# Moving the low-part subtraction of the expert weights from GpSimd to VectorE, and projecting the queries with split weights

## The chip, the core and the metric

The kernel runs on one core of one Trainium2 chip. Five engines work side by side, each through its own queue in order: TensorE (PE; its weight loads are listed apart, as PEld), VectorE (DVE), ScalarE (ACT), GpSimd (POOL) and SyncE (SP), which here only issues DMAs. The metric is the time of one execution in microseconds; lower is better.

## The reference, cut to what matters

Two transformer blocks are computed for 512 tokens of width 1024 in float32. The change is in the last part of the second one, `peer_ffn`, a layer with 16384 experts of one hidden unit each:

```python
q = _rms((xt @ w_q).reshape(T, P_HEADS, P_KEY_DIM)).astype(x.dtype)
s1 = jnp.einsum('thd,hnd->thn', q[..., :half], sub_keys[:, 0])
s2 = jnp.einsum('thd,hnd->thn', q[..., half:], sub_keys[:, 1])
v1, i1 = lax.top_k(s1, P_TOPK)
v2, i2 = lax.top_k(s2, P_TOPK)
cand = (v1[..., :, None] + v2[..., None, :]).reshape(T, P_HEADS, P_TOPK * P_TOPK)
vals, ci = lax.top_k(cand, P_TOPK)
...
a = jnp.einsum('cd,ckd->ck', xc, expert_u[ec])
w = (gc * jax.nn.gelu(a.astype(jnp.float32))).astype(x.dtype)
return jnp.einsum('ck,ckd->cd', w, expert_v[ec])
```

Each token has 8 heads x 16 chosen experts; the rows of expert_u and expert_v that they name are used.

## The kernel before, in words

Float32 weights are multiplied in two parts. `chunk` loads a 128x1024 tile of weights (`wraw`, three buffers), ACT copies it into a reduced format (`whi`, two buffers), and `wlo`, also with two buffers, takes what is left, wraw - whi: one subtraction, on DVE or on POOL by `lo_engine`. `mm3` then makes three matmuls of one product: whi with the high part of the activations, whi with their low part, wlo with the high part (lines L84 to L86). `up_tile` does this for one tile of expert_u ("pu", the first product, 128 experts): 24 matmuls of 384 columns, then Gelu on ACT.

`peer` has three stages that matter here.

- The queries (about 1012 to 1217 us): 16 half heads n. Query n is projected (`w3[n]`), copied by ACT, multiplied with its keys, and DVE searches the 16 best of each row (`top16`); after every second one, POOL and DVE form pairs and decode them (`pairs`, `decode`). From n = 4 on, tiles of the first product stand between the queries, two and one in turn, their low parts by POOL. Only query 0 is projected from split weights. For the others POOL adds the two parts of the activations into `whole` at the start, and the loaded weights are multiplied with it as they are (L1397).
- The gates (about 1217 to 1431): 30 further tiles of the first product, with one-hot matmuls between them that spread the gates of tokens 0 to 383 over all experts.
- The last stage (1431 to the end): step e of 128 multiplies tile e of expert_v ("pv", the second product, 18 matmuls of 512 columns into y) with the gated hidden values. In the first 80 steps a tile of the first product follows each. Beside this runs the work for the last 128 tokens, `gathered`: 256 rows-by-index DMAs (128 from expert_u, "pun", and 128 from expert_v) that POOL issues (L1493) into four buffers (`r4`), each of them then reduced or added by one DVE operation (L1498 for the first 128, L1508 for the rest).

The order of the instructions on every engine is set by a scheduler that simulates the engines. `fetch` puts each gather behind `self.pool_last`, the last subtraction that POOL was given, so that between 80 subtractions on POOL stand the gathers of each step.

Of the kernel before, what the change touches and what calls it, by code (L numbers as in the profile page):

```python
# [12 lines left out]
F32 = mybir.dt.float32  # L13
# [5 lines left out]
ALU = mybir.AluOpType  # L19
# [25 lines left out]
class Builder:  # L45
# [1200 lines left out]
    def peer(self, hd, xn, xd):  # L1246


        nc, tc, bp = self.nc, self.tc, self.bp
        NT = 384  # L1250
        AHEAD = 27
        AWAY = 21
        NREST = 4
        with ExitStack() as s5:
# [3 lines left out]
            T = lambda tag, bufs=1, dt=F32, shape=(128, 512): wk.tile(list(shape), dt, tag=tag, name=tag, bufs=bufs)  # L1258
# [4 lines left out]
            w3 = self.i["w3"]  # L1263
# [12 lines left out]
            def top16(out, ind, s, n):  # L1276
                rest = T("rest", NREST, shape=(128, 128))[:, :n]
                nc.vector.max(out[:, 0:8], s)
                nc.vector.match_replace(rest, out[:, 0:8], s, LOWEST)
                nc.vector.max(out[:, 8:16], rest)  # L1280
                nc.vector.max_index(ind[:, 0:8], out[:, 0:8], s)
                nc.vector.max_index(ind[:, 8:16], out[:, 8:16], rest)
# [16 lines left out]
            def pairs(hd8):  # L1299
                cand = T("oh2", 4, shape=(128, 4, 128))[:, :, :NC]  # L1300
                i = 0
                while i < 16:
                    m, n = sum(r == ROWS[i] for r in ROWS), ROWS[i]
                    sh = [128, 4, m, n]
                    v1 = val[:, :, hd8, 0, i:i + m]
                    v2 = val[:, :, hd8, 1, 0:n]
                    o = cand[:, :, START[i]:START[i] + m * n]
                    if m == 1:
                        v1 = v1.to_broadcast([128, 4, n])
                    elif n == 1:  # L1310
                        v2 = v2.to_broadcast([128, 4, m])
                    else:
                        o = o.rearrange("p b (m n) -> p b m n", n=n)
                        v1, v2 = v1[:, :, :, None].to_broadcast(sh), v2[:, :, None, :].to_broadcast(sh)
                    nc.gpsimd.tensor_tensor(o, v1, v2, op=ALU.add)
                    i += m
                for b in range(4):
                    top16(best[:, b, hd8], ci[:, b, hd8], cand[:, b], NC)
# [44 lines left out]
            def up_tile(e, lo_engine="pool"):  # L1363
                c = self.chunk(self.i["pu"][e], lo_engine=lo_engine)
                p = P()
                for k in range(8):
                    s = slice(k * 128, (k + 1) * 128)
                    self.mm3(p[:, :NT], (c[0][:, s], c[1][:, s]), (xn[0][k][:, :NT], xn[1][k][:, :NT]), k == 0, k == 7)
                away = e >= 128 - AWAY
                g = T("gs", 2, shape=(128, NT)) if away else T("gt", AHEAD, shape=(128, NT))  # L1370
                nc.scalar.activation(g, p[:, :NT], AF.Gelu_apprx_tanh)
                if away:
                    nc.sync.dma_start(ud[e - 128 + AWAY], g)
                else:
                    up[e] = g

            first_tiles = iter([*range(128 - AWAY, 128), *range(AHEAD)])


            whole = T("big", 2, shape=(128, 8, 512))  # L1380
            for k in range(8):
                nc.gpsimd.tensor_tensor(whole[:, k], xn[0][k], xn[1][k], op=ALU.add)

            for n in range(16):
                hd8, half = n // 2, n % 2
                with self.in_order(self.after if n < 2 else []):
                    if n % 4 == 0:
                        keys = T("r4", 4, shape=(128, 2, 512))[:, 0]
                        nc.sync.dma_start(keys, self.i["keys"][n // 4])
                    acc = P()  # L1390
                    if n == 0:
                        self.project(acc, self.chunk(w3[n], lo_engine="pool"), xn)
                    else:
                        w = self.wp.tile([128, 1024], F32, tag="wraw", name="wraw", bufs=3)
                        nc.sync.dma_start(w, w3[n])
                        for k in range(8):
                            nc.tensor.matmul(acc, w[:, k * 128:(k + 1) * 128], whole[:, k], start=k == 0, stop=k == 7)  # L1397
                q = T("r4", 4, shape=(128, 2, 512))[:, 0]
                nc.scalar.copy(q, acc)
                before, sq = sq, TP()  # L1400
                nc.scalar.activation(sq, acc, AF.Square)
                sp = P(f"y{(0, 1, 3, 4, 5)[n % 5]}")
                ks = slice(n % 4 * 128, n % 4 * 128 + 128)
                for b in range(4):
                    bs = slice(b * 128, b * 128 + 128)
                    nc.tensor.matmul(sp[:, bs], q[:, bs], keys[:, ks], start=True, stop=True)
                for b in range(4):
                    top16(val[:, b, hd8, half], idx[:, b, hd8, half], sp[:, b * 128:(b + 1) * 128], 128)
                if half == 1:
                    nc.gpsimd.tensor_tensor(sq, sq, before, op=ALU.add)  # L1410
                    for b in range(4):
                        nc.tensor.matmul(sv[:, b, hd8], sq[:, b * 128:(b + 1) * 128], self.ones[:, 0:2], start=True, stop=True)
                    pairs(hd8)
                    decode(hd8)
                for _ in range((0, 0, 0, 0, 2, 1)[min(n, 4 + n % 2)]):
                    up_tile(next(first_tiles))
# [116 lines left out]
            for e in range(128):  # L1533
                if e % 4 == 0:
                    w = T("big", 2, shape=(128, NT // 32, 4, 32))
                    n = NT // 32 - (e == 0)
                    load = nc.sync.dma_start(w[:, :n], wd[:n, :, e:e + 4, :].rearrange("g p e t -> p g e t"))
                    if e == 0:
                        with tc.issue_after(load.ins):
                            nc.sync.dma_start(wd[n], last[0])  # L1540
                c = self.chunk(self.i["pv"][e])
                hm = TP()[:, :NT]
                hv, uv = (t.rearrange("p (a t) -> p a t", t=32) for t in (hm, up[e]))
                nc.vector.tensor_tensor(hv[:, :n], uv[:, :n], w[:, :n, e % 4], op=ALU.mult)  # L1544
                if e < 4:
                    nc.vector.tensor_tensor(hv[:, n], uv[:, n], last[0][:, e], op=ALU.mult)
                del up[e]
                xh, xl = TP(F32R)[:, :NT], TP(F32R)[:, :NT]
                self.split_into(hm, xh, xl)
                for b in range(3):  # L1550
                    bs = slice(b * 128, b * 128 + 128)
                    for d in range(2):
                        cs = slice(d * 512, d * 512 + 512)
                        self.mm3(y[b][d], (xh[:, bs], xl[:, bs]), (c[0][:, cs], c[1][:, cs]), e == 0, e == 127)
                if e + AHEAD < both:
                    up_tile(e + AHEAD)
                if e + 2 >= both and e + 2 < 128:
                    up[e + 2] = T("gl", 3, shape=(128, NT))
                    nc.sync.dma_start(up[e + 2], ud[e + 2 - both])
                steps = both - AHEAD  # L1560
                work.advance((e + 1) / steps * 0.86 if e < steps else 0.86 + (e + 1 - steps) / 36 * 0.15)
# [106 lines left out]
```

## Time and profile before

| | us |
|---|---|
| three runs | 2383.24, 2383.82, 2390.1 (median 2383.82) |
| profiled execution | 2386.1 |
| its span, first to last instruction | 2384.1 |
| PE busy | 2261.5 (95%) |
| PE weight loads busy | 1906.0 (80%) |
| DVE busy | 1682.8 (71%) |
| POOL busy | 1001.5 (42%) |
| ACT busy | 1003.6 (42%) |
| mean rate of the DMAs | 182 GB/s; in the last stage near 290 |

PE's busy time is nearly the whole span, but it is made of stages with different limits, so the shares by themselves don't say what bounds one of them.

### The profile page before, as it was taken

How to read it: one execution, taken by the hardware profiler on the slowest of the kernel's cores; microseconds unless marked ns; L12 is line 12 of the kernel's file. 1: busy time of each engine (PE TensorE's matmuls, PEld its weight loads, DVE VectorE, ACT ScalarE, POOL GpSimd, SP SyncE). 2: the span in 40 equal slices, each digit the busy share in tenths (PEclk: the TensorE clock that was granted, in tenths of full speed). 3: DMA queues.
4: the chain of work that ended last, by engine and by line, in shares of the span. 5: the costliest groups of instructions: out<-in, count | busy, mean ns of one | idle time of the engine just before them, and what ended most of it. 6: DMA issues, size and time to landing. Idle time of an engine off the chain costs nothing.

```text
span 2384.1 us, 31933 instructions
## 1 busy us (share of the span) xinstructions
PE 2261.5 (95%) x11207; PEld 1906.0 (80%) x11207; DVE 1682.8 (71%) x3504; ACT 1003.6 (42%) x1766; POOL 1001.5 (42%) x829
## 2 busy tenths in 40 slices
PE   6999999999998889899999998999999999999999
PEld 4888888888886668767789998888888878877787
DVE  7766666533457887676789966777767877778875
ACT  4544444422344688622238762333333333323332
POOL 4221121000034657455520006767777767776410
PEclk9999999999999999899999999999999999999999
DMA  3222222333342122333345558988888988889984
GB/s 116 80 82 87 80 80 88 125 94 94 96 126 75 54 71 98 120 97 118 116 135 199 208 196 292 313 297 284 286 290 296 305 281 281 296 281 325 348 306 154
DMA packets 166833, 433.26 MB, mean 182 GB/s; under 512 B 14608, under 2 KB 69392, under 8 KB 165136
## 3 DMA queue, kind: packets, MB, share of 16 engines
q1 hardware_dynamic: 129808, 296.98, 38.5%
q0 software_dynamic: 36864, 134.23, 16.0%
q8 instruction: 88, 1.44, 0.3%
q14 instruction: 73, 0.60, 0.1%
HBM read 391.91 MB, written 38.21 MB: 180 GB/s over the span
## 4 chain that ended last, share of the span: by engine, by line
PE 70%; DVE 10%; DMA 9%; issue 5%; POOL 4%; ACT 2%; DVEq 0%; SPq 0%; POOLq 0%; ACTq 0%
PE mm L86 11%; PE mm L84 10%; PE mm L85 10%; DMA r<-pun_in,row 6%; PE y L85 4%; PE y L86 4%; PE y L1466 4%; PE mm L1397 3%; PE y L84 3%; POOL wlo L71 3%; PE g L86 2%; PE g L85 2%; PE g L84 2%; PE s L367 2%; DMA r<-pv_in,row 2%
## 5 line engine op out<-in xcount | busy, mean ns | idle before, releaser
L65 ACT CAST whi<-wraw 128x1024 fp32r<-128x1024 f32 (+2 forms) x398 | 414.1, 1041 | 742.3 <-PE y L86 281.3
L71 POOL TENSOR_TENSOR wlo<-wraw,whi 128x1024 fp32r<-128x1024 f32 (+3 forms) x124 | 311.6, 2514 | 649.7 <-ACT whi L65 648.5
L86 PE MATMUL mm<-uh,wlo 128*128 128x384 f32 (+1 forms) x1512 | 543.7, 360 | 6.8 <-POOL wlo L71 5.0
L84 PE MATMUL mm<-uh,whi 128*128 128x384 f32 (+1 forms) x1512 | 545.5, 361 | 4.4 <-ACT whi L65 4.1
L85 PE MATMUL mm<-ul,whi 128*128 128x384 f32 (+1 forms) x1512 | 539.9, 357 | 3.6 <-DVE ul L71 3.6
L71 DVE TENSOR_TENSOR wlo<-wraw,whi 128x1024 fp32r<-128x1024 f32 (+1 forms) x274 | 341.6, 1247 | 180.3 <-ACT whi L65 180.1
L85 PE MATMUL y<-wlo,p 128*128 128x512 f32 x768 | 306.9, 400 | 48.2 <-DVE wlo L71 48.0
L86 PEld LDWEIGHTS mm<-uh,wlo 128*128 128x128 f32 x1512 | 285.6, 189 | 36.4 <-POOL wlo L71 17.0
L84 PEld LDWEIGHTS mm<-uh,whi 128*128 128x128 f32 x1512 | 286.1, 189 | 29.8 <-ACT whi L65 4.5
L85 PEld LDWEIGHTS mm<-ul,whi 128*128 128x128 f32 x1512 | 286.0, 189 | 28.3 <-DVE ul L71 3.8
L1498 DVE CUSTOM_DVE_ANT_0 r<-r,val 128x1024 f32<-128x1024 f32 x128 | 226.2, 1783 | 110.0 <-DMA r<-pun_in,row 109.1
L86 PE MATMUL y<-whi,p 128*128 128x512 f32 x768 | 301.3, 393 | 0.0
L1508 DVE SCALAR_TENSOR_TENSOR idx<-r,act,idx 128x1024 f32<-128x1024 f32 x127 | 211.0, 1661 | 76.4 <-DMA r<-pv_in,row 74.9
L1493 POOL DMA_INDIRECT r<-pv_in,row x128 | 189.7, 1482 | 81.4 <-DVE idx L1508 44.7
L85 PEld LDWEIGHTS y<-wlo,p 128*128 128x128 f32 x768 | 144.8, 189 | 97.8 <-DVE wlo L71 67.4
L1493 POOL DMA_INDIRECT r<-pun_in,row x128 | 187.5, 1465 | 42.2 <-issue 20.6
L84 PE MATMUL y<-whi,p 128*128 128x512 f32 x768 | 197.6, 392 | 0.0
L65 ACT CAST p<-p 128x384 fp32r<-128x384 f32 x128 | 65.8, 514 | 292.3 <-DVE p L1544 290.7
L86 PEld LDWEIGHTS y<-whi,p 128*128 128x128 f32 x768 | 144.9, 189 | 30.0
L84 PEld LDWEIGHTS y<-whi,p 128*128 128x128 f32 x768 | 143.0, 188 | 25.3 <-ACT whi L65 0.5
L372 ACT ACTIVATE p<-p,st 128x128 f32<-128x128 f32 (+3 forms) x160 | 89.6, 561 | 71.5 <-DVE st L371 70.6
L1463 DVE TENSOR_SCALAR r<-iota,iT,iT 128x128 f32<-128x128 f32 x384 | 104.6, 342 | 19.9 <-PE y L1466 19.9
(605 smaller groups left out, 3763.0 us busy)
## 6 DMA issues: line engine op xcount, KB each, us to landing
wraw<-w_in SPq DMA_DIRECT2D x145, 512.0 KB, 3.5
wraw<-pu_in SPq DMA_DIRECT2D x128, 512.0 KB, 5.5
wraw<-pv_in SPq DMA_DIRECT2D x128, 512.0 KB, 5.0
wd<-big SPq DMA_DIRECT2D x12, 2048.0 KB, 7.3
big<-wd SPq DMA_DIRECT2D x31, 768.0 KB, 6.1
hd<-h SPq DMA_DIRECT2D x24, 256.0 KB, 2.2
h<-hd SPq DMA_DIRECT2D x16, 256.0 KB, 3.7
ud<-gs SPq DMA_DIRECT2D x21, 192.0 KB, 2.0
```

Of the source, the lines that this page charges most:

```text
L65: nc.scalar.copy(hi, src)
L71: i = eng.tensor_tensor(lo, src, hi, op=ALU.subtract)
L84: mm(out, w[0], x[0], start=start, stop=False)
L85: mm(out, w[0], x[1], start=False, stop=False)
L86: mm(out, w[1], x[0], start=False, stop=stop)
L372: nc.scalar.activation(pi, pi, AF.Exp, bias=st[:, 0:1], scale=-1.0, accum_out=st[:, 1:2])
L1397: nc.tensor.matmul(acc, w[:, k * 128:(k + 1) * 128], whole[:, k], start=k == 0, stop=k == 7)
L1463: nc.vector.tensor_scalar(hot[:, 0, t], iota, i1, g, op0=ALU.is_equal, op1=ALU.mult)
L1466: nc.tensor.matmul(wp[:, t * 128:(t + 1) * 128], hot[:, 0, t], hot[:, 1, t], start=True, stop=True)
L1493: nc.gpsimd.indirect_dma_start(t, None, src, bass.IndirectOffsetOnAxis(ap=rows[n][:, s:s + 1], axis=0))
L1498: nc.vector.tensor_tensor_reduce(t, t, xn3, 1.0, 0.0, ALU.mult, ALU.add, act[:, s:s + 1])
L1508: nc.vector.scalar_tensor_tensor(yg[0], t, act[:, s:s + 1], yg[0], op0=ALU.mult, op1=ALU.add)
```

## The change

In the last stage the subtraction for the first product's tiles goes to DVE. All 16 queries are projected from split weights, with the low part on POOL for queries 0 and 1 and on DVE for the others; `whole`, its eight additions and the matmuls with whole weights go.

```diff
-            whole = T("big", 2, shape=(128, 8, 512))
-            for k in range(8):
-                nc.gpsimd.tensor_tensor(whole[:, k], xn[0][k], xn[1][k], op=ALU.add)
...
                     acc = P()
-                    if n == 0:
-                        self.project(acc, self.chunk(w3[n], lo_engine="pool"), xn)
-                    else:
-                        w = self.wp.tile([128, 1024], F32, tag="wraw", name="wraw", bufs=3)
-                        nc.sync.dma_start(w, w3[n])
-                        for k in range(8):
-                            nc.tensor.matmul(acc, w[:, k * 128:(k + 1) * 128], whole[:, k], start=k == 0, stop=k == 7)
+                    self.project(acc, self.chunk(w3[n], lo_engine="pool" if n < 2 else "dve"), xn)
...
                 if e + AHEAD < both:
-                    up_tile(e + AHEAD)
+                    up_tile(e + AHEAD, "dve")
```

The scheduler orders all engines anew. Three places show it; in the changed kernel L1482 is the gather that was L1493, L1487 the operation that was L1498, L1533 the product of hidden values and gates that was L1544, L1526 and L1529 are the loads and the last store of the gates that were L1537 and L1540.

POOL's queue early in the last stage, before:

```order
L1493 DMA r_13877<-pun_in,row_13505 128x1024
L1493 DMA r_13880<-pun_in,row_13505 128x1024
L1493 DMA r_13883<-pun_in,row_13505 128x1024
L71 TENSOR_TENSOR wlo<-wraw,whi 128x1024
L1493 DMA r_13949<-pun_in,row_13505 128x1024
L1493 DMA r_13952<-pun_in,row_13505 128x1024
L1493 DMA r_13955<-pun_in,row_13505 128x1024
L71 TENSOR_TENSOR wlo<-wraw,whi 128x1024
```

The same queue of the changed kernel:

```order
L1482 DMA r_14168<-pun_in,row_13796 128x1024
L1482 DMA r_14171<-pun_in,row_13796 128x1024
L1482 DMA r_14174<-pun_in,row_13796 128x1024
L1482 DMA r_14240<-pun_in,row_13796 128x1024
L1482 DMA r_14243<-pun_in,row_13796 128x1024
```

The subtractions are gone and with them the place that bound a gather to its step; gathers follow each other.

DVE's queue in the middle of the gathers from expert_u, about one step of the last stage, before (one wlo a step, for pv; the rows that write only act read out a sum; p<-gt,big makes the hidden values, p<-p their low part):

```order
L71 TENSOR_TENSOR wlo<-wraw,whi 128x1024
L1498 ISA r_14956,act<-r_14956,val 128x1024
L1498 ISA act 128x1
L1498 ISA r_14959,act<-r_14959,val 128x1024
L1498 ISA act 128x1
L71 TENSOR_TENSOR p<-p 128x384
L1544 TENSOR_TENSOR p<-gt,big 128x384
```

The same of the changed kernel:

```order
L71 TENSOR_TENSOR wlo<-wraw,whi 128x1024
L1487 ISA r_15824,act<-r_15824,val 128x1024
L1487 ISA act 128x1
L71 TENSOR_TENSOR wlo<-wraw,whi 128x1024
L1487 ISA r_15890,act<-r_15890,val 128x1024
L1487 ISA act 128x1
L71 TENSOR_TENSOR p<-p 128x384
L1533 TENSOR_TENSOR p<-gt,big 128x384
L1487 ISA r_15893,act<-r_15893,val 128x1024
```

A second subtraction per step, for pu, stands between the gather operations, most with one of them ahead of it.

SP's queue where the last stage begins, before (wd holds the gates in memory; big is a tile of them for four steps):

```order
L1540 DMA wd<-big 128x4096
L94 DMA wraw<-pv_in 128x1024
L1537 DMA big<-wd 128x12x128 x2
L94 DMA wraw<-pu_in 128x1024
L94 DMA wraw<-pv_in 128x1024
```

The same of the changed kernel:

```order
L1529 DMA wd<-big 128x4096
L94 DMA wraw<-pv_in 128x1024
L94 DMA wraw<-pu_in 128x1024
L1526 DMA big<-wd 128x12x128 x2
L94 DMA wraw<-pv_in 128x1024
```

One load of pu weights has moved ahead of the two loads of gates.

## Rows read from the trace of the kernel before

**Rows 1.** Busy time by stretch: length, PE, PEld, DVE, ACT, POOL, clock, DMA, GB/s.

```profile
1012.00:1217.00 205.00, 202.16 (x858) 142.30 (x857) 149.48 (x793) 46.40 (x69) 105.40 (x111) 0.99 0.35 110
1217.00:1431.00 214.00, 214.00 (x1516) 213.81 (x1515) 184.89 (x566) 149.74 (x266) 7.65 (x11) 1.00 0.55 194
1500.00:2150.00 650.00, 603.89 (x2954) 528.61 (x2953) 493.40 (x519) 208.14 (x283) 470.89 (x264) 1.00 0.87 291
2200.00:2300.00 100.00, 97.76 (x423) 78.72 (x422) 83.51 (x100) 35.77 (x48) 39.99 (x26) 1.00 0.96 342
```

**Rows 2.** Instructions of line 84: duration min/median/max in ns, first and last start.

```profile
L84 PE MATMUL mm<-uh,whi x1512: 331/335/795, 39.9 to 2172.9; 128*128 128x384 f32 x128, 128*128 128x512 f32 x61
...
L84 PE MATMUL y<-whi,p x768: 387/392/498, 1431.5 to 2375.3; 128*128 128x512 f32 x192
```

**Rows 3.** The chain that ended last: start, us, what.

```profile
1119.95 6.87 PE mm L1397 x16
...
2304.28 1.37 PE y L84 x6
2308.40 1.37 PE y L84 x6
```

**Rows 4.** Timeline of PE in one tile of the first product, every third matmul.

```profile
1966.76 0.33 PE L86 MATMUL mm<-uh,wlo 128*128 128x384 f32 x1
...
1967.28 0.33 PE L86 MATMUL mm<-uh,wlo 128*128 128x384 f32 x1
```

**Rows 5.** Waits from 1432 to 2190: total us, times, longest.

```profile
POOL wlo L71 <- ACT whi L65: 318.3, 47, 188.1
...
DVE r L1498 <- DMA r<-pun_in,row: 109.1, 64, 6.2
DVE idx L1508 <- DMA r<-pv_in,row: 71.9, 44, 3.5
PEld y L85 <- DVE wlo L71: 62.3, 39, 2.7
...
PEld mm L86 <- POOL wlo L71: 17.0, 34, 1.9
```

**Rows 6.** Groups by line from 1432 to 2190: busy us, mean ns, idle before.

```profile
L71 POOL TENSOR_TENSOR wlo<-wraw,whi 128x1024 fp32r<-128x1024 f32 x80 | 213.4, 2668 | 319.5 <-ACT whi L65 318.3
```

**Rows 7.** Instructions of line 1498: duration min/median/max in ns.

```profile
L1498 DVE CUSTOM_DVE_ANT_0 r<-r,val x128: 1209/1226/3623, 1441.9 to 1870.0; 128x1024 f32<-128x1024 f32 x128
```

**Rows 8.** Groups by line from 2195 to 2300, after the first product's last tile.

```profile
L1508 DVE SCALAR_TENSOR_TENSOR idx<-r,act,idx 128x1024 f32<-128x1024 f32 x31 | 39.6, 1279 | 3.0 <-DMA r<-pv_in,row 3.0
```

**Rows 9.** Costliest groups of the whole span, from the page.

```profile
L1498 DVE CUSTOM_DVE_ANT_0 r<-r,val 128x1024 f32<-128x1024 f32 x128 | 226.2, 1783 | 110.0 <-DMA r<-pun_in,row 109.1
...
L1508 DVE SCALAR_TENSOR_TENSOR idx<-r,act,idx 128x1024 f32<-128x1024 f32 x127 | 211.0, 1661 | 76.4 <-DMA r<-pv_in,row 74.9
```

**Rows 10.** Timeline of POOL and DVE at two places: start, us, instruction.

```profile
1475.53 3.62 DVE L1498 CUSTOM_DVE_ANT_0 r<-r,val 128x1024 f32<-128x1024 f32 x1 [0.71 <-DMA r<-pun_in,row]
1475.64 2.43 POOL L71 TENSOR_TENSOR wlo<-wraw,whi 128x1024 fp32r<-128x1024 f32 x1
...
1966.46 1.21 DVE L71 TENSOR_TENSOR wlo<-wraw,whi 128x1024 fp32r<-128x1024 f32 x1
1966.74 1.74 POOL L1493 DMA_INDIRECT r<-pv_in,row  x1 [0.30 <-DVE p L1544]
1968.79 0.94 POOL L1493 DMA_INDIRECT r<-pv_in,row  x1 [0.31 <-PE mm L86]
```

**Rows 11.** DMA issues, 1431 to 2190, then 2195 to 2290: median us to landing.

```profile
r<-pun_in,row POOLq DMA_INDIRECT x128, 6.6
...
r<-pv_in,row POOLq DMA_INDIRECT x28, 8.5
```

**Rows 12.** Timeline of ACT where the last stage begins.

```profile
1456.32 1.04 ACT L65 CAST whi<-wraw 128x1024 fp32r<-128x1024 f32 x1 [6.22 <-DMA wraw<-pu_in]
```

**Rows 13.** Groups by line while the queries are projected, 1012 to 1217.

```profile
L71 POOL TENSOR_TENSOR wlo<-wraw,whi 128x1024 fp32r<-128x1024 f32 x18 | 42.5, 2364 | 26.3 <-ACT whi L65 26.3
```

## The prediction

> **What bounds the kernel now.** I read stretches first, then the waits inside the stretch that the change touches. In each row of [rows 1] stand the length, the busy us of TensorE (PE), of its weight loads, VectorE (DVE), ScalarE (ACT) and GpSimd (POOL), then granted clock, DMA share and GB/s. Where the queries are projected (1012 to 1217 us) PE is busy 202 of 205 us; in the next stage (1217 to 1431), which the change leaves alone, 214 of 214. So a microsecond that PE saves on the queries ends the stage after it a microsecond sooner, as long as nothing else becomes late.
>
> The last stage begins with the first product into y at 1431.5. Its first 80 steps each hold 24 matmuls of 384 columns (one tile of the first product, "pu") and 18 of 512 columns (one of the second, "pv"); the last pu matmul is at 2172.9 [rows 2]. That is 741.7 us, 9.27 a step. What PE needs for a step: six matmuls of 512 columns take 1.37 us in the chain, 18 take 4.11 (an undisturbed pv step late in the kernel goes from 2304.28 to 2308.40, 4.12) [rows 3]; three of 384 columns take 0.52 [rows 4], 24 take 4.16. Together 8.27, for 80 steps 662 us. So 80 us of these steps are not matmul pace. PE is in fact busy only 604 of 650 us there, and at 291 GB/s and 0.87 of the DMA engines the memory isn't full either [rows 1].
>
> Who keeps PE waiting stands in the waits of this stretch [rows 5]: first DVE's low part of the pv weights, 62.3 us at the weight loads; POOL's low part of the pu weights, 17.0. DVE is late because of the gathers: it stood 109.1 and 71.9 us waiting for gathered rows. These are late because POOL, which issues them in order with its 80 subtractions, stood 318.3 us before a subtraction whose ScalarE copy wasn't there (188 of it one wait ahead of the stage), with gathers behind it in its queue. And each subtraction is long: 2.67 us [rows 6].
>
> The second loss is a collision. The gather operation of the first half of DVE's list (L1498) has a median of 1.226 us [rows 7], that of the second (L1508) takes 1.279 late in the stage, where POOL only issues [rows 8]; their means over the stage are 1.783 and 1.661 [rows 9]. The differences, 0.56 and 0.38 us, times 128 and 127, are 120 us of DVE time. One pair shows where it goes: L1498 takes 3.62 us from 1475.53, and POOL's 2.43 us subtraction begins in it at 1475.64 [rows 10]: 1.21 us of work and 2.41 of standing.
>
> **The change, the last stage.** POOL loses 80 subtractions, 213 us [rows 6], and nothing of POOL's is left between gathers: as the order shows, they follow each other. DVE gains 80 subtractions of 1.21 us [rows 10], 97 us, and gets back up to 120 us of standing, as POOL's remaining work there is issuing, beside which L1508 takes its 1.279 us [rows 8].
>
> DVE's step is then (counted in DVE's order, 230 gather operations stand ahead of the 80th step's end, where 209 stood: 2.88 a step) 2.88 x 1.31 (L1498 with its 0.08 us read-out), two subtractions, 2.42, and two short operations of 0.55: 7.3 us, 88% of PE's 8.27. It fits, but PE's pu weights now stand in the same queue as the gathers.
>
> Whether the gathers come in time: four r buffers go round. Now a round takes 4 x 741.7/209 = 14.2 us. Without POOL's subtractions it is an issue of 1.74 us when DVE is busy (0.94 when idle) [rows 10], a landing of 6.6 us, or 8.5 as it was late in the stage at a DMA share of 0.96 [rows 1, 11], DVE's 1.3, and 0.3 between issues: 9.9 to 11.8. At 2.88 gathers a step that asks for 7.1 to 8.5 us a step. So PE's 8.27 and the ring's 8.5 are nearly the same, and nothing else asks for more: 2.75 MB a step (two weight tiles, a quarter of a 768 KB load, 2.88 gathers of 512 KB) at the 342 GB/s of [rows 1] are 8.0 us.
>
> Bounds for a step: 8.27 below; above, 9.27 plus what it costs if the pu weights come as late as the pv weights do (62.3 us in place of POOL's 17.0): 9.83. I take 8.45, by the row that it is nearest to: 2200 to 2300, where DVE already makes every low part at the same pace of a chunk each 4.1 us, DMA is at 0.96, and PE is busy 97.8% [rows 1]; 8.27/0.978 = 8.46. Of the start of the stage I keep 4 us: PE stood there while ScalarE waited for a pu weight load until 1456.32 (6.2 us) [rows 12]; SP now issues one pu load ahead of two large loads, which may shorten it. 80 x 8.45 + 4 = 680 against 741.7: -62 us (bounds -80 and +45). The remaining 48 pv steps ran from 2173 to just past 2375.3 [rows 2], 4.2 a step against 4.12; they have 25 gathers now instead of 46: -2 us.
>
> **The change, the queries.** A whole-weight product of one query is 16 pieces and 6.87 us in the chain [rows 3]; split, it is 24 matmuls at 1.37/6, 5.48. Fifteen times 1.39 is 20.9 us of PE saved. Added are 15 copies of 1.04 us on ACT (46 of 205 us busy), 14 subtractions of 1.21 on DVE (149 of 205) and one on POOL, less eight additions there: each has room [rows 1]. But the queries now share the two whi and two wlo buffers with the pu tiles between them, where before they took none. A copy can begin only when the tile before the preceding one is multiplied, so copy and subtraction must fit in the preceding tile's 4.16 us: 1.04 + 1.21 on DVE does, 1.04 + 2.36 on POOL [rows 13] just does, if neither stands in its queue; ahead of DVE's now stand top-16 searches, ahead of POOL's the decoding. Fully covered: -20.9. Nothing covered: 15 x 2.25 = 34 on top, +13. I take -13, nearer to the covered end, since both sums fit into 4.16 us and DVE would be at 166 of 187 us.
>
> The sum: -62 - 2 - 13 = -77. The profiled execution took 2386.1 us (span 2384.1 and 2.0 around it), 2.3 over the median of 2383.8; from the median, 2307.
>
> **A rule against the row.** The issue of a gather takes 1.74 us from 1966.74, during DVE's subtraction (1966.46), and 0.94 from 1968.79, when DVE waits [rows 10]. The Trainium skill, SBUF — State Buffer, section "Who interferes with whom", says that a VectorE instruction with two SBUF inputs contends with a GpSimd one that reads SBUF, and infers that descriptor generation, which writes, is spared by tensor_tensor. By that every issue would stay at 0.94, and the ring would ask for 6.5 to 7.9 us a step instead of 7.1 to 8.5; the row disagrees with the inference, and I go by the row.
>
> **Rivals.**
> *The ring decides.* With DVE busier, issues longer and landings at 8.5 us or more, the four r buffers take 12.4 us a round: 8.9 a step, 716 with the start, -26; with -2 and -13 2343. For it: the DMA share rises. Against: late in the stage landings of 8.5 us cost DVE almost no waiting, though at fewer gathers.
> *DVE's queue takes POOL's place.* Every pu and pv subtraction now stands behind a gather operation; if gathers stay 1 us late, PE loses on two waits half of what it lost on one. The 80 steps stay at 742, and -13 - 2 leaves 2369. For it: 88% load in order. Against: what made gathers late was POOL's queue.
> *The queries pay.* Copy and subtraction uncovered, +13 in place of -13: 2333. For it: two buffers. Against: 4.16 us to hide 2.3 or 3.4.
> *Slower.* If DVE waits for gathers ahead of both low parts, so that PE loses 62.3 us a second time and only POOL's 17.0 go, that is +45, and with nothing from the queries 2429. It decides from the point where gathers reach DVE more than 1.9 us late, the room that copy (1.04) and subtraction (1.21) leave in 4.16. Against it: DVE's own standing of 120 us goes.
>
> **How the numbers follow.** Forecast 0.62 (its own range 2290 to 2330), ring 0.13, DVE's queue 0.11, queries 0.06, slower 0.06, no change 0.02. The forecast, the ring and the queries hold 0.81: from 2288 (steps nearly at 8.27 and the queries covered: -80 - 2 - 21 would be 2281) to 2350. About 0.3%, 7 us, is what a measurement of this kernel can tell. Faster: all but the last two cases, 0.91 with some doubt at 2369; within 0.3%: 0.03; slower 0.06.
>
> **What would show it.** The first 80 steps near 680 us; means of L1498 and L1508 near their medians; POOL without subtractions in the last stage; DVE's wait for gathers far below 181 us; landings of 7 to 9 us; DMA share near 0.95. In the queries, 24 matmuls in 5.5 us with few waits for wlo. It is wrong if PE waits for DVE's low part of pu as long as it did for pv's, or if DVE still waits over 150 us for gathers.

## The result and the profile after

The changed kernel took 2298.18 us (median; 2294.41 to 2301.9) beside 2383.53 us of the kernel before on the same chip: a ratio of 0.9639, 95% interval 0.9611 to 0.9667. The forecast was 2307 with a range of 2288 to 2350. The profiled execution took 2294.41, its span is 2292.6.

Busy time by stretch of the changed kernel, columns as in [rows 1]: the queries, the gates, the first 20 us of the last stage, and most of its first 80 steps.

```profile
1012.00:1200.00 188.00, 182.54 (x984) 165.69 (x983) 166.58 (x805) 59.76 (x85) 102.30 (x103) 0.99 0.37 115
1200.00:1410.00 210.00, 210.00 (x1489) 209.77 (x1488) 183.74 (x561) 147.18 (x262) 11.14 (x14) 1.00 0.56 199
1410.00:1430.00 20.00, 14.41 (x63) 13.19 (x62) 9.29 (x20) 5.40 (x8) 6.46 (x6) 0.83 0.95 352
1500.00:2060.00 560.00, 559.47 (x2828) 509.22 (x2827) 466.54 (x571) 197.38 (x270) 261.90 (x202) 1.00 0.95 340
```

In the steps PE is now busy 559.5 of 560 us, where it was 603.9 of 650: nothing keeps it waiting any more. DVE is busy 83%. The instructions of line 84 in the changed kernel, as in [rows 2]:

```profile
L84 PE MATMUL mm<-uh,whi x1632: 332/336/796, 39.5 to 2087.7; 128*128 128x384 f32 x114, 128*128 128x512 f32 x68
...
L84 PE MATMUL y<-whi,p x768: 387/392/395, 1412.5 to 2283.6; 128*128 128x512 f32 x192
```

The last stage begins at 1412.5, 19.0 us sooner. Its 80 steps last until the start of the last matmul at 2087.7: 675.2 us against 741.4 in [rows 2] (the prediction's 741.7 counts that matmul too), 66.2 less. What comes after them takes 204.9 us (to the span's end, 2292.6) against 211.2: 6.3 less. Together 91.5 us, the difference of the spans; the medians differ by 85.4, since the execution profiled before (2386.1) lay 2.6 us above the median here and that after 3.8 below.

The pace of a step stands in the chain that ended last, as in [rows 3]:

```profile
1506.12 1.37 PE y L84 x6
...
1514.42 1.37 PE y L84 x6
```

8.30 us, PE's own 8.27 with 0.03 on top. The waits of the changed kernel from 1413 to 2088 (total us, times, longest), as in [rows 5]:

```profile
POOL r L1482 <- DVE act L1487: 188.2, 104, 6.6
...
POOL r L1482 <- DVE idx L1497: 151.2, 88, 4.2
...
DVE r L1487 <- DMA r<-pun_in,row: 14.3, 12, 4.3
...
PEld mm L86 <- DVE wlo L71: 9.0, 4, 5.9
...
DVE idx L1497 <- DMA r<-pv_in,row: 2.5, 3, 1.6
```

DVE waits 16.8 us for gathered rows instead of 181, and the 62.3 us in which PE waited for the pv low part are gone. Now POOL waits for DVE to free the r buffers (339 us): the gathers are ahead of their user. Groups by line in the same stretch, as in [rows 6, 9]:

```profile
L71 DVE TENSOR_TENSOR wlo<-wraw,whi 128x1024 fp32r<-128x1024 f32 x160 | 195.7, 1223 | 78.8 <-ACT whi L65 78.6
...
L1487 DVE CUSTOM_DVE_ANT_0 r<-r,val 128x1024 f32<-128x1024 f32 x127 | 153.5, 1219 | 14.3 <-DMA r<-pun_in,row 14.3
...
L1497 DVE SCALAR_TENSOR_TENSOR idx<-r,act,idx 128x1024 f32<-128x1024 f32 x113 | 144.6, 1280 | 3.2 <-DMA r<-pv_in,row 2.5
```

The gather operations take 1219 and 1280 ns, their undisturbed times in [rows 7, 8], instead of 1783 and 1661. DVE's 80 further subtractions (98 us at 1223 ns) cost less than the 120 us of standing that it got back.

What is left stands at the start of the stage. PE's two waits there in the changed kernel, and DVE in the same moment:

```profile
1422.68 0.69 PE L86 MATMUL mm<-uh,wlo 128*128 128x384 f32 x1 [5.59 <-DVE wlo L71]
...
1451.97 0.44 PE L86 MATMUL mm<-uh,wlo 128*128 128x384 f32 x1 [1.68 <-DVE wlo L71]
```

```profile
1420.25 1.23 DVE L1487 CUSTOM_DVE_ANT_0 r<-r,val 128x1024 f32<-128x1024 f32 x1 [4.29 <-DMA r<-pun_in,row]
...
1421.40 1.22 DVE L71 TENSOR_TENSOR wlo<-wraw,whi 128x1024 fp32r<-128x1024 f32 x1
```

The pu low part stands behind a gather operation whose rows came 4.29 us late, and PE stands 5.59 us behind both: the price of sharing DVE's queue with the gathers. It happens once at this size. The DMA engines are 95% busy in these 20 us, among others with a store of gates that was issued at 1409.10 and took 10.5 us; that this load made the rows late is argued and not shown.

### The profile page after: what moved, and what is told of

Its sections match the earlier page's. It is cut to its first block, busy times and chain, and to the rows that moved or that the text cites. A ratio compares the mean times of both kernels' runs of the same rounds, so it can differ in the third digit from the quotient of the medians.

```text
span 2292.6 us, 32166 instructions
## 1 busy us (share of the span) xinstructions
PE 2220.0 (97%) x11327; PEld 1934.7 (84%) x11327; DVE 1673.3 (73%) x3598; ACT 1013.8 (44%) x1781; POOL 744.1 (32%) x742
## 4 chain that ended last, share of the span: by engine, by line
PE 85%; DVE 10%; ACT 2%; DMA 1%; issue 1%; POOL 1%; SPq 0%; DVEq 0%; POOLq 0%; ACTq 0%
PE mm L86 13%; PE mm L84 12%; PE mm L85 12%; PE y L85 7%; PE y L84 7%; PE y L86 7%; PE y L1455 4%; PE g L86 3%; PE g L85 3%; PE g L84 3%; PE s L367 2%; PE pt L393 2%; DVE wlo L71 2%; PE o L397 1%; PE o L396 1%
## 5 line engine op out<-in xcount | busy, mean ns | idle before, releaser
L71 DVE TENSOR_TENSOR wlo<-wraw,whi 128x1024 fp32r<-128x1024 f32 x368 | 460.7, 1252 | 262.6 <-ACT whi L65 262.4
L86 PE MATMUL mm<-uh,wlo 128*128 128x384 f32 (+1 forms) x1632 | 587.9, 360 | 14.0 <-DVE wlo L71 11.5
L85 PE MATMUL mm<-ul,whi 128*128 128x384 f32 (+1 forms) x1632 | 587.9, 360 | 3.3 <-DVE ul L71 3.3
L84 PE MATMUL mm<-uh,whi 128*128 128x384 f32 (+1 forms) x1632 | 588.9, 361 | 0.3 <-DVE ul L144 0.3
L86 PEld LDWEIGHTS mm<-uh,wlo 128*128 128x128 f32 x1632 | 308.8, 189 | 40.6 <-DVE wlo L71 15.4
L85 PEld LDWEIGHTS mm<-ul,whi 128*128 128x128 f32 x1632 | 309.0, 189 | 29.6 <-DVE ul L71 3.6
L1482 POOL DMA_INDIRECT r<-pun_in,row x128 | 165.0, 1289 | 372.9 <-DVE act L1487 183.5
L1482 POOL DMA_INDIRECT r<-pv_in,row x128 | 167.7, 1310 | 188.2 <-DVE idx L1497 168.1
L71 POOL TENSOR_TENSOR wlo<-wraw,whi 128x1024 fp32r<-128x1024 f32 (+3 forms) x45 | 104.7, 2331 | 326.3 <-ACT whi L65 326.2
L85 PEld LDWEIGHTS y<-wlo,p 128*128 128x128 f32 x768 | 144.2, 188 | 32.2 <-DVE wlo L71 0.7
L1487 DVE CUSTOM_DVE_ANT_0 r<-r,val 128x1024 f32<-128x1024 f32 x128 | 154.7, 1219 | 15.3 <-DMA r<-pun_in,row 15.3
L1497 DVE SCALAR_TENSOR_TENSOR idx<-r,act,idx 128x1024 f32<-128x1024 f32 x127 | 162.5, 1280 | 3.2 <-DMA r<-pv_in,row 2.5
L71 DVE TENSOR_TENSOR p<-p 128x384 fp32r<-128x384 f32 x128 | 71.3, 557 | 85.9 <-PE y L85 82.4
```

Of the source, the lines that this page charges most:

```text
L71: i = eng.tensor_tensor(lo, src, hi, op=ALU.subtract)
L84: mm(out, w[0], x[0], start=start, stop=False)
L85: mm(out, w[0], x[1], start=False, stop=False)
L86: mm(out, w[1], x[0], start=False, stop=stop)
L1482: nc.gpsimd.indirect_dma_start(t, None, src, bass.IndirectOffsetOnAxis(ap=rows[n][:, s:s + 1], axis=0))
L1487: nc.vector.tensor_tensor_reduce(t, t, xn3, 1.0, 0.0, ALU.mult, ALU.add, act[:, s:s + 1])
```

## The experiments

"Steps" means the time from the first y product to the last matmul of the first product, read as in [rows 2]: 741.4 us before, 675.2 after. Ratios are to the kernel before, with 95% intervals.

**The two parts apart.** e1_last_stage_only is the kernel before with the first line below; e2_queries_only is the changed kernel with the second.

```diff
-                    up_tile(e + AHEAD)
+                    up_tile(e + AHEAD, "dve")
```

```diff
-                    up_tile(e + AHEAD, "dve")
+                    up_tile(e + AHEAD)
```

> The kernel before with the last stage's subtraction on DVE alone; the queries stay as they were. Two independent parts: 80 steps near 675 us as in the changed kernel, start of the last stage near 1431, in all 70 to 73 us faster than before (near 2312). If the two parts help each other (the freed big buffer, the earlier start): under 60 us.

> The changed kernel with POOL's subtraction back in the last stage. Matmul columns as the cause: first product into y near 1412, 80 steps again near 742, 19 us faster than before (near 2365). If the earlier start shifts work into a busier last stage: under 10 us.

e1: 2313.56 us, 0.971 [0.9683, 0.9736], steps 678.4. e2: 2358.42 us, 0.991 [0.988, 0.9941], steps 730.8, the means of the gather operations 1775 and 1678 as before. The gains, 2.9 and 0.9%, add up to the whole 3.6% within their intervals. So the 80 subtractions make about three quarters of the gain, the queries the rest. e1 came out as expected; the steps of e2 are 10.6 us shorter than before, where the same 742 was expected, and no run shows why.

**The gathers not bound to POOL's subtraction.** The kernel before, with this edit in `fetch`: the scheduler may put a gather ahead of any subtraction.

```diff
-                    with tc.issue_after(self.pool_last):
+                    with self.in_order([]):
```

> The kernel before, with POOL's subtractions, but no gather is put behind a step's subtraction any more. If the binding to the step was what made gathers late: DVE's wait for gathered rows falls from 181 us to under 60 and 40 us or more are won (near 2340). If POOL's long subtractions and their collision with DVE are the cause: means of DVE's gather operations stay near 1.7 us, the 80 steps stay over 720 us, at most 15 us are won.

2369.39 us, 0.9943 [0.9922, 0.9964], steps 735.7. The waits of e3_gathers_unbound from 1432 to 2180:

```profile
PEld mm L86 <- POOL wlo L71: 61.2, 63, 3.6
...
DVE r L1498 <- DMA r<-pun_in,row: 32.8, 23, 4.3
...
DVE idx L1508 <- DMA r<-pv_in,row: 29.6, 18, 3.0
...
PEld y L85 <- DVE wlo L71: 3.1, 2, 1.9
```

The gathers come in time (62.4 us of waiting, 181 before), PE's wait for the pv low part is gone (3.1, before 62.3), and in its place PE waits 61.2 us for POOL's pu low part, now late itself behind the gathers. Freeing the gathers alone moves the wait to the other product. The means of the gather operations fell part of the way, to 1429 and 1415 ns, which neither expectation had.

**The gathers bound to DVE's subtraction.** The kernel before with the last stage's subtraction on DVE, and `pool_last` set to that subtraction (the line's index moves by one).

```diff
-        if lo_engine == "pool":
+        if lo_engine == "pool" or self.binding:
             self.pool_last = i.ins
```

> The kernel before with the last stage's subtraction on DVE, and every gather put behind that DVE subtraction in the scheduler's order, as it stood behind POOL's. If the binding was the cause: DVE waits over 100 us for gathers and under 30 us are won. If the subtraction's place on POOL was the cause: near the kernel with the last-stage part alone, 60 us or more won.

2314.56 us, 0.9713 [0.9688, 0.9739], steps 677.6: like e1, and it had to be. The traces of e1 and e4 hold the same instructions in the same order on every engine, so the edit bound nothing (the gathers stand in POOL's queue, the subtraction in DVE's). The run is a second measurement of e1 and says nothing of the binding; e14 below tests that.

**The ring of r buffers.** The changed kernel with three buffers instead of four, in all five places that use them; one is shown.

```diff
-                    t = T("r4", 4, shape=(128, 1024))
+                    t = T("r4", 3, shape=(128, 1024))
```

> The changed kernel with three r buffers in place of four. If a round of the buffers is what it was reckoned to be (issue 1.3, landing 6.6 to 7.5, operation 1.3, 0.3 between: 9.5 to 10.4 us), three ask for 9.1 to 10.0 us a step at 2.88 gathers: 80 steps of 730 to 800 us, 55 to 125 us slower than the changed kernel's 675. If gathers have ample room: within 7 us of the changed kernel.

2351.49 us, 0.9877 [0.9831, 0.9922], steps 721.3, 9.02 us each; DVE waits 146 us for gathers from 1432 to 2130. That is a little under the 730 to 800 expected of a tight ring, and far from ample room. If the ring sets the pace here, a round is 3 x 9.02 / 2.88 = 9.4 us, and four buffers then ask for 6.8 us a step: room to 8.3.

**The subtraction made twice.** The changed kernel, in the last stage with a second, equal subtraction of the pu tile on DVE (L97).

```diff
+        if twice:
+            nc.vector.tensor_tensor(lo[:, :n], raw[:, :n], hi[:, :n], op=ALU.subtract)
```

> The changed kernel with each of the 80 pu subtractions of the last stage made twice on DVE (98 us of DVE work more, same result). If DVE is near its end (83% busy in the 80 steps, 98% with this): PE waits for low parts, 80 steps of 690 to 735 us, 15 to 60 us slower. If DVE has more room than its busy time says: under 7 us slower.

2417.58 us, 1.0153 [1.0119, 1.0187], steps 800.0: far from every expectation. PE in one step of e8_subtract_twice:

```profile
1700.67 0.33 PE L84 MATMUL mm<-uh,whi 128*128 128x384 f32 x1
1700.84 0.34 PE L85 MATMUL mm<-ul,whi 128*128 128x384 f32 x1
1701.96 1.67 PE L84 MATMUL y<-whi,p 128*128 128x512 f32 x6 [0.79 <-ACT whi L65]
1703.47 0.33 PE L86 MATMUL mm<-uh,wlo 128*128 128x384 f32 x1
```

The scheduler, reckoning with a later low part, drew six products of the next pv tile into the pu tile, after its second matmul. Their whi can be copied only when the pv tile before is done, so PE stands at them in 61 of the 80 steps, 85.7 us in all at the weight loads. In the kernels before and after, and in the other experiments on the last stage, PE's order there is the same but for a few rows. So this run tells of another order of PE, and nothing of how much more DVE could carry.

**More work on DVE, not ahead of a low part.** The changed kernel with two additions per step whose sums nobody reads; they leave PE's order as it is but for a few rows.

```diff
                     up_tile(e + AHEAD, "dve")
+                    for _ in range(2):
+                        g = up[e + AHEAD]
+                        nc.vector.tensor_tensor(T("dead", shape=(128, NT)), g, g, op=ALU.add)
```

> The changed kernel with two additions per step on DVE whose sums nobody reads (128x384, both inputs the step's Gelu tile), 160 at about 0.55 us, 88 us, spread between the gather operations and not ahead of a low part as the second subtraction of e8_subtract_twice was. If DVE's time is what the step has no more of (the queue in order has less room than its 83% busy say): the steps grow by 65 us or more, the kernel to 2360 or more. If e8_subtract_twice was slow because the low part itself came 1.2 us later: the steps grow by less than 30, the kernel stays below 2330.

2300.66 us, 0.9648 [0.9622, 0.9674], steps 677.7. Busy time by stretch of e12_dve_work_in_step:

```profile
1500.00:2050.00 550.00, 549.37 (x2774) 499.15 (x2774) 514.64 (x696) 199.24 (x266) 255.82 (x198) 1.00 0.95 339
```

DVE is busy 514.6 of 550 us, 94%, and PE stands only 0.6 us in all. So DVE's load wasn't what limits the changed kernel.

**Work on POOL that nobody waits for.** The changed kernel with three such additions per step on POOL. A first form, e10_idle_pool_work, took other tiles, ready from the start:

```diff
+                    with tc.issue_after(self.dve_last):
+                        for _ in range(3):
+                            nc.gpsimd.tensor_tensor(T("dead", shape=(128, 384)), xn[0][0][:, :384], xn[1][0][:, :384], op=ALU.add)
```

> The changed kernel with three additions of 128x384 on POOL in each of the 80 steps whose results nobody reads (about 2.9 us a step, as long as the subtraction that left). If the collision of POOL's work with DVE's two-input operations is the cause of the loss before: means of DVE's gather operations rise to 1.6 us or more, DVE's work passes 95% of a step, 20 us or more slower. If it was that PE and the gathers waited for POOL's results and queue: under 10 us slower, though the means rise.

It missed its place: as in e4, an order behind an instruction of DVE didn't bind POOL's queue, and the additions ran from 1014 to 1423, ahead of the last stage. The steps stayed at 675.8 (gather operations 1221 and 1281 ns). The kernel took 2432.92 us, 1.0222 [1.0189, 1.0256], because the stage ahead became slow: from 1200 to 1400 PE was busy only 155.9 of 200 us, at a clock of 0.74, beside POOL at 185 and DVE at 194. The second form takes the step's Gelu tile:

```diff
                     up_tile(e + AHEAD, "dve")
+                    for _ in range(3):
+                        g = up[e + AHEAD]
+                        nc.gpsimd.tensor_tensor(T("dead", shape=(128, NT)), g, g, op=ALU.add)
```

> The changed kernel with three additions per step on POOL whose sums nobody reads (128x384, both inputs the step's Gelu tile, so they can't run before their step): 240 at about 1.1 us, 265 us, more than the 213 of the subtractions taken away. PE's order is that of the changed kernel and no engine waits for them; they stand between POOL's gathers. If POOL's two-input work beside DVE's is the cost, whoever reads it: the means of the two gather operations rise from 1219 and 1280 to 1600 or more, DVE stands 120 us or more, and the 80 steps go from 675 to 770 or more, the kernel to 2390 or more. If the cost lay in PE waiting for a low part that POOL makes: the steps stay below 700, the kernel below 2325.

2362.27 us, 0.9902 [0.9876, 0.9928], steps 744.5, 69 more than without. Groups by line of e11_pool_work_in_step from 1432 to 2080, and its busy time by stretch:

```profile
L71 DVE TENSOR_TENSOR wlo<-wraw,whi 128x1024 fp32r<-128x1024 f32 x141 | 203.7, 1445 | 9.9 <-ACT whi L65 9.4 <-PE y L86 0.5
...
L1487 DVE CUSTOM_DVE_ANT_0 r<-r,val 128x1024 f32<-128x1024 f32 x124 | 172.7, 1404 | 7.8 <-DMA r<-pun_in,row 7.7
...
L1497 DVE SCALAR_TENSOR_TENSOR idx<-r,act,idx 128x1024 f32<-128x1024 f32 x87 | 136.1, 1565 | 3.6 <-DMA r<-pv_in,row 2.9
...
L1533 DVE TENSOR_TENSOR p<-gt,big 128x384 f32<-128x384 f32 x70 | 86.6, 1237 | 0.0
```

```profile
1500.00:2050.00 550.00, 517.31 (x2522) 454.48 (x2521) 534.10 (x523) 178.24 (x241) 462.74 (x360) 0.99 0.88 307
```

Every two-input operation of DVE is longer (L1533 1237 ns, 551 in the changed kernel), DVE is busy 97%, and it hardly waits for gathers (10.6 us). So the collision by itself, with no engine waiting for POOL's result, makes DVE the bound and costs 69 us. The result lies between the two expectations, nearer to the first: the means rose less than its 1600 ns, and the steps by less than its 95 us, but far past the 700 us of the second. The 240 additions are 247 us of POOL's time in all, where the 80 subtractions were 213.

**Every second subtraction on POOL.** The changed kernel with:

```diff
-                    up_tile(e + AHEAD, "dve")
+                    up_tile(e + AHEAD, "dve" if e % 2 else "pool")
```

> The changed kernel with the low part of every second pu tile of the last stage back on POOL (40 of 80). If the cost of a subtraction on POOL is by the piece (its collision with DVE and the gathers behind it): half of the 55 to 60 us that all 80 cost, the steps at 700 to 708, the kernel at 2322 to 2335. If it takes a queue that never comes free (threshold): the steps below 685, the kernel at 2298 to 2308, perhaps below the changed kernel, since DVE is relieved of 49 us.

2397.41 us, 1.0068 [1.0041, 1.0095], steps 777.2: both expectations fell, half the subtractions cost more than all 80. DVE waits 166 us for gathers from 1432 to 2080, and PE 30.4 us for POOL's low part and 47.8 for DVE's at the weight loads. In POOL's order five or six gathers now follow each subtraction, where three did; that their rows come late in such groups is the likely reason, argued and not shown.

**The wait in POOL's queue without the work.** The changed kernel; POOL also subtracts 8 of the 1024 columns of each pu tile, for nobody, and the gathers are put behind it.

```diff
+        elif self.small is not None:
+            j = nc.gpsimd.tensor_tensor(self.small, src[:, :8], hi[:, :8], op=ALU.subtract)
+            self.pool_last = j.ins
```

> The changed kernel, and in every step of the last stage POOL also subtracts 8 of the 1024 columns of the pu tile, from the same tiles as it did before the change, into a tile that nobody reads; the gathers are put behind this as they were behind the whole subtraction. So POOL's queue stands again before ScalarE's copy with the gathers behind it (it stood 318 us in the kernel before), but there is hardly a collision (about 0.2 us of work in place of 2.67) and PE waits for nothing of POOL's. If the waiting in POOL's queue made the gathers late, as the prediction had it: DVE waits 100 us or more for gathers, the 80 steps take 700 to 735 us, the kernel 2320 to 2355. If it was the 2.67 us beside DVE (standing and lateness both): DVE waits below 40 us for gathers, the steps stay within 675 to 690, the kernel within 2295 to 2315.

2378.08 us, 0.9984 [0.9964, 1.0004], steps 759.6: the whole gain of the last stage is lost. The steps are longer than the 700 to 735 that were expected of late gathers. Waits of e14_queue_only from 1432 to 2150, and its two gather operations (L1492 and L1502 there) by line:

```profile
POOL dead L77 <- ACT whi L67: 299.8, 76, 10.4
...
DVE r L1492 <- DMA r<-pun_in,row: 111.3, 55, 6.0
...
DVE idx L1502 <- DMA r<-pv_in,row: 79.4, 39, 4.4
...
PEld y L90 <- DVE wlo L73: 67.4, 35, 4.2
```

```profile
L1492 DVE CUSTOM_DVE_ANT_0 r<-r,val 128x1024 f32<-128x1024 f32 x125 | 152.6, 1222 | 111.5 <-DMA r<-pun_in,row 111.3
...
L1502 DVE SCALAR_TENSOR_TENSOR idx<-r,act,idx 128x1024 f32<-128x1024 f32 x83 | 106.5, 1283 | 79.6 <-DMA r<-pv_in,row 79.4
```

The gather operations keep their undisturbed 1222 and 1283 ns, so there is no collision to speak of. Yet POOL stands 299.8 us before ScalarE's copies with the gathers behind it, DVE waits 190.7 us for rows, and PE 67.4 us for the pv low part: for these two the picture of [rows 5] to within 10 us. POOL's own wait is longer than it was. Of the 318.3 us in [rows 5] one wait of 188.1 ended as the stage began, so 130.2 lie in the stage, beside 213.4 of subtracting [rows 6]: 344 us in which gathers stood behind a subtraction. Here it is 299.8 and 60.4 (80 at 0.755), 360 us. So e14 puts into the wait what before was mostly the subtraction itself. What the tiny subtraction reads holds nobody up (ScalarE's copies wait for PE, not for POOL). That the step is even longer than before (9.5 against 9.27) fits DVE's 98 us of further subtractions, which delayed nothing as long as gathers came in time.

**Gathers asked for later at the start.** The changed kernel; the gathers' pace in the first steps is to be set back.

```diff
-                work.advance((e + 1) / steps * 0.86 if e < steps ...
+                work.advance((e - 2) / (steps - 3) * 0.86 if e < steps ...
```

> The changed kernel with the gathers' work begun three steps later and then a little faster. The wait at the start of the last stage, 5.6 us for a low part that stands behind a gather operation waiting for its rows, goes: 5 to 8 us faster than the changed kernel (near 2291). If the stage's start is bound by the loads of gates and weights instead: no difference.

2299.03 us, 0.9665 [0.9631, 0.9699], steps 677.7. PE's stall at the start stayed (6.2 us in place of 5.59). But the edit missed its aim: POOL issued the first five gathers from 1402.4 to 1412.9, in the changed kernel from 1402.6 to 1412.5. So it isn't shown whether later gathers, or less traffic beside them, would clear the stall. No version here beats the changed kernel.

## Why the prediction was right, point by point

**The steps, -62 forecast, -66.2 measured.** Two terms were off and cancelled. The steady step runs at 8.30 us, not at the 8.45 taken from PE's 97.8% in [rows 1]; PE stood in that row, 2.2 us of it for DVE's low part, which from 1500 to 2060 it no longer does. In turn the start keeps more than the 4 us reckoned: 675.2 - 80 x 8.30 = 11 us, of which PE's two waits above are 7.3; the granted clock of 0.83 from 1410 to 1430, a mean over its levels of 2.4 and 1.2 GHz in a stretch in which PE stood, goes the same way.

**Late gathers, the first cause.** Right: e14 shows that in the changed kernel POOL's wait for ScalarE's copy, with gathers behind it, is enough to lose all that the steps had gained. How much of the lateness before came from that wait (130 us in the stage) and how much from the subtraction behind it (213 us) isn't separated. e3 shows that it can't be cured by order alone while the subtraction stays on POOL.

**The collision, the second cause.** Right in size where it was counted: the means fell to the undisturbed times, 0.56 x 128 + 0.38 x 127 = 120 us. And e11 shows that a collision can be enough too, in the changed kernel, whose DVE has 98 us more to do. What the prediction left unsaid is how the two stand to each other: they aren't two terms of a sum. Put back one at a time, the wait costs 84 us (759.6 - 675.2) and the collision 69, while both together, with 98 us less for DVE to do, made the 66.2 of the kernel before. That the change gained so much because it removed both at once is likely and not shown: e3, which freed the gathers, won 5.7 us of the steps, but no run took the collision alone out of the kernel before.

**DVE's load, 88% forecast.** The forecast added up durations, and added up in that way DVE's rows from 1500 to 2060 come to 498.9 of 560 us, 89%. The 83% above is the time in which at least one of them ran; each begins some 0.08 us before the last one's end (1421.40 and 1420.25 + 1.23 above). So the forecast held, and the rival in which DVE's queue takes POOL's place had less for it than it seemed: at 94% (e12) nothing is lost. The sharper condition was the other one named there, whether gathers come in time.

**The ring, 7.1 to 8.5 us a step forecast.** Nearer to the low end: 6.8 by e5, where rows landed after 6.8 and 6.6 us (medians); in the changed kernel they take 7.8 and 7.3 (from 1412 to 2088), so a round is some 0.9 us longer and the ring asks for (9.4 + 0.9) x 2.88 / 4 = 7.4. The rival in which it decides took the long issue and the slow landing for every gather.

**The rule against the row.** The row held. Issues of 0.93 to 1.98 us stand in the changed kernel, and their timeline shows what decides. POOL, then DVE, around 1520:

```profile
1520.79 1.67 POOL L1482 DMA_INDIRECT r<-pun_in,row  x1 [1.07 <-DVE act L1487]
1523.63 0.94 POOL L1482 DMA_INDIRECT r<-pun_in,row  x1 [1.16 <-DVE act L1487]
```

```profile
1520.44 1.22 DVE L71 TENSOR_TENSOR wlo<-wraw,whi 128x1024 fp32r<-128x1024 f32 x1
...
1523.72 1.23 DVE L71 TENSOR_TENSOR wlo<-wraw,whi 128x1024 fp32r<-128x1024 f32 x1 [0.36 <-ACT whi L65]
```

The first issue begins in a subtraction that has 0.87 us to go, and ends 0.80 us after it. The second begins 0.09 us ahead of a subtraction and takes 0.94 beside it. So it is with the rest of the timeline from 1500 to 2080: 137 of 208 issues began while a DVE operation ran and took 1.48 us on average (the operation had 0.68 to go, so they ended 0.80 after it); the other 71 took 0.93 to 0.95, though in 54 of them a DVE operation began. The Trainium skill's inference (SBUF — State Buffer, "Who interferes with whom") that tensor_tensor spares descriptor generation doesn't hold for these gathers. An earlier sentence of that section of the Trainium skill, that a VectorE instruction with two SBUF inputs contends with a GpSimd one that reads SBUF, agrees if the issue counts as one that reads (it takes its row numbers from a tile); that is argued.

**The queries, -13 forecast, -19.0 measured.** Mis-sized, and less so than it looks. Of the 19.0 us, 2.3 lie ahead of the queries, where both kernels do the same: the first matmul of query 0 starts at 1008.30 before and at 1005.98 after. So the queries and the gates won 16.7. From 1012 to the start of the last stage PE stood 2.8 us before and 5.5 after, all of the latter for low parts (3.0 us for DVE's, 2.5 for POOL's); the loss is 2.6, where I kept back 8 of the 20.9. The other 1.6 stay open. Over all runs the last stage begins between 1427.6 and 1433.0 with the queries of before, and with the new ones, e10 aside, between 1411.3 and 1415.0.

**The rest, -2 forecast, -6.3 measured.** Mis-sized: 14 gather operations were left after the last pu matmul instead of 38, where I counted 25 and 46, and PE's waits there fell from 4.6 us to 0.3.

**The slower rival.** It didn't happen here, but a part of its mechanism does exist: in e14 and e13, with late gathers, PE waits at the weight loads for both low parts that DVE makes (67.4 and 12.2 us in e14, 32.2 and 15.6 in e13), and the steps are 759.6 and 777.2. What makes the gathers late in e14 is POOL's queue, not DVE's.

## What to carry to other kernels

A subtraction on a lightly loaded engine is not priced by its duration: look at what stands behind it in that queue while it waits for its input (here gathers, behind 130 us of waiting and 213 of subtracting), and at what its operands do to the neighbour's operations (here 120 us of VectorE). Where two causes are named for one loss, put each back by itself into the faster kernel: each can be enough, and then removing one may give next to nothing, as in e3. Compare the order of every engine with that of the kernel it came from, too: e4 changed nothing and e9 not what it was meant to. And read the order of the bounding engine in each experiment before its time, since an extra operation can move a scheduler's order and cost more than itself, as in e8.

## What the runs showed of the hardware that was not expected

A gather's issue on GpSimd that begins while a two-input VectorE operation runs ends about 0.80 us after that operation (137 issues in the changed kernel); by itself it takes 0.94 us, and one that begins first isn't disturbed by an operation that begins in it (54 issues). A GpSimd subtraction of 8 columns shows the same in e14: 0.20 us where no VectorE operation ran (20 of 80), and otherwise until 0.06 us after that operation's end in nearly all cases, 0.755 on average over all. VectorE ran its queue in order at 94% busy while TensorE stood 0.6 of 550 us in the steady steps (e12).
